# Index queries and keys placed inside SBUF instead of by way of DRAM, in a two-layer hybrid decoder trunk

## The chip, the core and the metric

The kernel runs on one core of a Trainium2 chip. The metric is device time in microseconds (us) of one execution. A core has TensorE (PE: matrix products; its weight loads are shown apart as PEld), VectorE (DVE), ScalarE (ACT), GpSimd (POOL) and SyncE (SP, whose queue issues nearly all transfers here), and sixteen DMA engines that move the data. SBUF is the memory on the core with 128 partitions (rows), PSUM the one that TensorE writes, DRAM the memory outside.

## The reference, cut to what matters

One sequence of 1024 tokens of width 1024 passes two layers. Layer 0 mixes tokens by sparse attention, layer 1 by a short gated convolution; each is followed by a SwiGLU. The part that the change touches is the sparse attention:

```python
q, k = rope(rmsnorm(q)), rope(rmsnorm(k))      # 16 query heads, 4 key heads of 64
qi, ki = rope(qi), rope(layernorm(ki))         # 8 index heads of 64, one index key
s = einsum('bqhd,bsd->bqhs', qi, ki)
score = einsum('bqhs,bqh->bqs', relu(s), wi)   # causal
_, sel = top_k(score, 256)
o = softmax(q . k[sel] / 8) . v[sel]           # per query
```

The rotation (rope) works on the two halves of 32 numbers of each head: `x1*cos - x2*sin` and `x2*cos + x1*sin`. Everything is float32.

## The kernel before, in words

**Who orders the work.** The program is recorded as operations with priorities (`plan.pri`) and costs, and `Plan.drain` (line 392) then acts as a planner: it simulates the five engines and emits, engine by engine, the ready operation of the smallest priority. Each engine executes its own list in that order, so an operation that is late holds all that stand behind it on its engine. Transfers are issued by SP, also in order. `Plan.cost` (line 207) books a transfer from SP at 0.475 us of SP time, or 0.65 us when both ends are SBUF tiles, plus 1.6 us and its bytes at 380 GB/s until it has landed. These are bookings of the planner and no measurements. What depends on what is noted for each tile, or for each named part of a tile (`part_of`). Nearly all instructions are recorded by one helper and bear its line, L244, in the profile, so one goes by tile names.

**Stages.** The attention projections run up to about 311 us, block-wise attention up to about 640 us, and the tail (class `Tail`: feed-forward layers, convolution, output) from there to the end at 2306 us.

**Projections** (`Attention.project`, line 916). Products are made at float32 accuracy from three products of split operands (`whi` and `wlo`, split by ACT and DVE from `raw`, a ring of two weight buffers of 512 KB). `rope_pair` (line 996) makes two PSUM tiles of 128 rows for four heads: tile `two` = 0 has the first halves of the heads (4 heads x 32 rows), tile 1 the second halves, 512 tokens wide (one "half" of the sequence). ACT moves them to SBUF tiles `rt` (a ring of five), and DVE rotates them. The work goes in this order: the index key (`kist`, slot 0 of the tile `karena`), the index queries in four steps (half, pair) = (0,0), (0,1), (1,1), (1,0), the keys for both halves, the queries in four pairs by two halves, the values.

**From the rotated tiles to their places.** A product needs a whole head, 64 numbers, along the partitions, while a rotated tile has 32 rows of each of four heads. So `to_dram` (line 1029) stores the tile in DRAM, 32 rows to each head's place, and a load brings it back:

- Index queries go to `qid` (8 stores of up to 256 KB). `index` (line 1100) loads, for each block of 128 queries from block 2 on, all 8 heads into a half slot of `karena` (slots 1 to 3, 6 loads of 256 KB). It waits for all four stores of its half. The products with `kist` then run for two heads at once (rows 0 to 63 and 64 to 127), ACT takes the positive part from PSUM (`ps_L`) to tiles `s`, and DVE adds them up with their weights to the scores `sc`.
- Keys go to `kd` (4 stores). `load_k` (line 1092) loads them twice, to rows 0 to 63 and to rows 64 to 127 of slots 4 to 7 of `karena` (2 loads of 1 MB), after both halves are stored.
- Queries go to `qd` (16 stores). `attend` (line 1207) loads one block of 128 queries into `qst` (8 loads of 512 KB), one block ahead.

**Selection** (`select`, line 1141) finds the 256th score of each row by a search of 31 steps that ACT (`junk`) or DVE count alternately for two pairs of blocks; the planner puts its steps into gaps of the projections and of attention.

**Attention** (`attend`): for each block and pair of heads, scores on PE, masking and maximum on DVE, exponentials on ACT, transposes and products with values on PE. Beside it run steps of the adaLN projections (`adaw`, 256 KB loads).

**Tail.** `Tail.norm_stat` (line 1415) sums the squares for a norm into a tile `nss` of 4 numbers per partition, from the pool of the `u` tiles. The pool `top` (line 497) holds one unused number per partition at the upper end of SBUF, above the weight pool.

Of the kernel before, what the change touches and what calls it, by code (L numbers as in the profile page):

```python
# [450 lines left out]
P = 128  # L451
# [35 lines left out]
class Trunk:  # L487
# [3 lines left out]
    def __init__(self, plan):  # L491
        self.plan = self.nc = plan
        self.cp = Pool(plan, "const")
        self.pp = Pool(plan, "ps", space=PSUM)
        self.pa = Pool(plan, "pa", space=PSUM)
        self.pg = Pool(plan, "pg", space=PSUM)
        self.top = Pool(plan, "top", side="right")
        self.top.tile([P, 1], F32, name="top")
        self.wp = Pool(plan, "w", side="right", bufs=2)


# [85 lines left out]
    def setup(self, c, positions, ada_b, n1, n2, conv_w, gq, gk, lg, lb, rope_c, arenas, kgb, freq):  # L587
# [2 lines left out]
        nc.gpsimd.memset(ident, 1.0)  # L590
        nc.gpsimd.affine_select(ident, ident, pattern=[[-1, P]], compare_op=ALU.is_equal,
                                fill=0.0, base=0, channel_multiplier=1)
        self.blk4 = cp.tile([P, 4], F32, name="blk4")
        nc.vector.memset(self.blk4, 0.0)
        for i in range(4):
# [161 lines left out]
def trunk_kernel(tc, x, c, positions, ada_w, ada_b, norm1_g, norm2_g, attn_w_in, attn_q_norm_g,  # L757
                 attn_k_norm_g, idx_k_ln_g, idx_k_ln_b, attn_w_out, conv_w_in, conv_w,
                 conv_w_out, ffn_w_gate, ffn_w_up, ffn_w_down, rope_c, out):
    plan = Plan(tc.nc, tc)  # L760
    with ExitStack() as ctx:
        ctx.enter_context(tc.manual_schedule())
        tk = Trunk(plan)
        for p in (tk.cp, tk.pp):
            plan.open(p, ctx)
        xspill = [[plan.wrap(tc.dram_tile([P, HW], F32, name="xs%d_%d" % (i, d)), [P, HW])
                   for d in range(KT)] for i in range(NH)]
        a = Attention(tk, attn_w_in[0], attn_w_out[0], ada_w, xspill)
        a.first_norm(x, positions, lambda v: tk.setup(
            c, positions, ada_b, norm1_g, norm2_g, conv_w, attn_q_norm_g, attn_k_norm_g,  # L770
            idx_k_ln_g, idx_k_ln_b, rope_c, v, a.score[2][:, 256:384], a.score[4][:, HW:HW + 1]))
        a.project()
        a.attend()
        f = Tail(tk, ada_w, xspill)
        a.attended(f)
        f.run(ffn_w_gate, ffn_w_up, ffn_w_down, conv_w_in[0], conv_w_out[0], out)
        right, proj, left = (ctx.enter_context(ExitStack()) for _ in range(3))
        for p in (tk.top, tk.wp):
            plan.open(p, ctx)
        for p, stack in ((tk.pa, left), (a.kp, left), (a.keep, right), (a.sel, right),  # L780
                         (a.hp, proj), (a.pj, proj)):
            plan.open(p, stack)
        plan.drain(a.hp, a.pj)
        proj.close()
        plan.open(a.op, right)
        plan.open(a.at, left)
        plan.drain(a.kp, a.at, tk.pa)
        left.close()
        for p in (tk.pg, *f.first):
            plan.open(p, left)  # L790
        plan.drain(a.keep, a.sel, a.op)
        right.close()
        for p in f.second:
            plan.open(p, left)
        plan.drain()


class Attention:
# [3 lines left out]
    def __init__(self, tk, w, w_out, ada_w, xspill):  # L802
# [4 lines left out]
        def dram(name, shape):  # L807
            return plan.wrap(plan.tc.dram_tile(shape, F32, name=name), shape)

        self.qd = dram("qd", [HEADS * HD, T])  # L810
        self.qid = dram("qid", [IH * HD, T])
        self.kd = dram("kd", [KVH * HD, T])
        self.rd = dram("rd", [2, 4, 32, T // 4])
        self.kp = Pool(plan, "k4")
        self.keep = keep = Pool(plan, "keep", side="right")
# [17 lines left out]

    def arena(self, i):

        return self.karena.part_of(i)[:, i]

    def s4(self):
        return self.sel.tile([P, T], F32, name="s4", tag="s4", bufs=3)
# [76 lines left out]
    def project(self):  # L916
        tk, nc, sp, plan = self.tk, self.nc, self.pj, self.plan
        self.kist = self.arena(0)
        self.ssk = sp.tile([P, TB, KVH], F32, name="ssk", bufs=1)
        self.wiT = sp.tile([P, TB, IH], F32, name="wiT", bufs=1)  # L920
        s = 0
# [12 lines left out]
        for half, j in ((0, 0), (0, 1), (1, 1), (1, 0)):  # L934
            self.unit(s)
            if (half, j) != (1, 1):
                w = tk.wpair(self.w, C_QI + j * 2 * P)
            ts = slice(max(0, FREE_BLK * P - half * HW), HW)
            ab, sl, e = self.rope_pair(w, half, ts, None, None, s)
            s += (e - s) * (ts.stop - ts.start) / HW  # L940
            for two in range(2):
                self.to_dram(ab[two], self.qid, j, two, half, sl)
            if (half, j) == (0, 1):
                ends += self.indexed(s, (2, 3))
        self.free_bias()
# [6 lines left out]
        for half in range(NH):  # L952
# [3 lines left out]
                           self.ssk[:, half * 4:half * 4 + 4].rearrange("p a b -> p (a b)"),  # L956
                           1.0 / HD, sp.tile([P, 64], F32, name="rst", tag="rst8"))
            self.k_out(ab, rk, half, sl)
        self.load_k()
        for j in range(HEADS // 4):  # L960
            self.unit(s)
            w = tk.wpair(self.w, j * 2 * P)
            for half in range(NH):
                ab, sl, s = self.rope_pair(w, half, slice(0, HW), 0,
                                           self.ssq[:, :, 4 * j:4 * j + 4], s)
                for two in range(2):
                    self.to_dram(ab[two], self.qd, j, two, half, sl)
        self.unit(s)
        tk.rsqrt_small(self.qsc.rearrange("p a b -> p (a b)"),
                       self.ssq.rearrange("p a b -> p (a b)"), 1.0 / HD,  # L970
# [55 lines left out]
        tk.rotate(ab, tmp, self.C[:, sl], self.S[:, sl])  # L1026
        return ab, sl, s

    def to_dram(self, t, dram, j, two, half, sl):
        rows = dram.part_of((half, j, two))[2 * P * j:2 * P * (j + 1), sl]  # L1030
        self.nc.sync.dma_start(rows.rearrange("(h a q) t -> a h q t", a=2, q=32)[two], t)


    def ki_chain(self, kw):
        tk, nc, sp = self.tk, self.nc, self.pj
        n = HD + IH
# [43 lines left out]
    def k_out(self, ab, rk, half, sl):  # L1080
# [6 lines left out]
            nc.tensor.transpose(bc[:, blk(i)], rb[:, blk(i)], tk.ident)  # L1087
        for two in range(2):
            nc.vector.tensor_tensor(ab[two], ab[two], bc, op=ALU.mult)
            self.to_dram(ab[two], self.kd, 0, two, half, sl)  # L1090

    def load_k(self):

        src = self.kd.rearrange("(g d) t -> d g t", d=HD)
        dst = self.karena.part_of(list(range(KVH, 2 * KVH)))
        for r in (0, HD):
            self.nc.sync.dma_start(dst[r:r + HD, KVH:], src)


    def index(self, b, n):  # L1100
        tk, nc = self.tk, self.nc
        wd = (b + 1) * P
        q = self.karena.part_of((1 + n // 2, n % 2))[:, 1 + n // 2, half_of(n % 2)].rearrange(
            "p (h t) -> p h t", t=P)
        src = self.qid.part_of([(b // 4, j, two) for j in range(2) for two in range(2)])
        nc.sync.dma_start(q, src[:, blk(b)].rearrange("(h p) t -> p h t", p=P))
        sc = self.score[b]
        for hp in range(IH // 2):
            rs = [self.s4()[:, 0:wd] for _ in range(2)]
            self.pair_products(q[:, hp], self.kist, wd, lambda r, cs, ps: nc.scalar.activation(  # L1110
                rs[r][:, cs], ps, AF.Relu))
            for i, r in enumerate(rs):
                wi = self.wiT[:, b, 2 * hp + i:2 * hp + i + 1]
# [93 lines left out]
    def attend(self):  # L1207
# [4 lines left out]
        for b in range(TB):  # L1212
            if b % 2 == 0:
# [3 lines left out]
            plan.pri = t0 - 12.0  # L1217
            q = (self.at if b % 2 else self.keep).tile([P, T], F32, name="qst", tag="qst",
                                                       bufs=1).rearrange("p (h t) -> p h t", t=P)
            nc.sync.dma_start(q, self.qd[:, blk(b)].rearrange("(h p) t -> p h t", p=P))  # L1220
            for g in range(KVH):
                for _ in range((0, 0, 2, 2, 4, 4, 4, 4)[b]):
                    plan.pri = t0 + (t1 - t0) * g / 4.0
# [133 lines left out]
class Tail:  # L1357
# [57 lines left out]
    def norm_stat(self, half, tag="sm"):  # L1415
# [3 lines left out]
        for d in range(KT):  # L1419
# [2 lines left out]
            if d:  # L1422
                nc.vector.tensor_tensor(sq, acc, sq, op=ALU.add)
            acc = sq
        ps, ss = self.tk.ps(tag), self.up.tile([P, 4], F32, name="nss", tag="nss", bufs=2)
        for t in range(4):
            nc.tensor.transpose(ps[:, blk(t)], acc[:, blk(t)], self.tk.ident)
        nc.vector.tensor_reduce(ss, ps.rearrange("p (a b) -> p a b", b=P), axis=AX.X, op=ALU.add)
# [450 lines left out]
```

## Time and profile before

| what | before |
|---|---|
| median of three runs | 2315.85 us (2315.74 to 2316.34) |
| the profiled execution | 2307.38 us |
| its span, first to last instruction | 2305.7 us |
| mean granted TensorE clock | 0.986 |
| PE / DVE / ACT busy | 96% / 83% / 49% |
| DMA | 356.35 MB, mean 155 GB/s |

The profile shows one execution. A row of a group has the engine, the operation, the tile written and the tiles read, the shape and the count. In brackets stands the time for which the engine sat idle before it, with what ended that wait. Rows of the queue "SPq" are issues of transfers, and their length is that of the issue, not of the transfer. Rows by windows give, for each stretch of time, the busy time of each engine with the number of instructions in brackets, then the granted TensorE clock (1.00 is full speed), the share of the sixteen DMA engines that is busy, and what they move in GB/s. The chain is the sequence of work and waits that ended last, followed back from the end.

### The profile page before, as it was taken

What the parts mean: (1) busy time and instruction counts of PE and PEld (TensorE: products, weight loads), DVE (VectorE), ACT (ScalarE), POOL (GpSimd) and SP (SyncE); (2) the same over time, 40 slices, a digit from 0 to 9 for tenths busy, and PEclk for the clock granted to TensorE, in tenths of its full rate; (3) what the DMA queues carried; (4) which work ended last, traced back from release to release, by engine and by line L of the source; (5) the groups of instructions that cost most, each with busy time, mean ns of one, the idle gap of its engine ahead of it and who ended that gap; (6) DMA issues with size and microseconds to landing.
All of it is one profiled execution on the core that took longest, in us unless ns stands there. A gap on an engine that the chain in (4) does not pass through costs nothing.

```text
span 2305.7 us, 32524 instructions
## 1 busy us (share of the span) xinstructions
PE 2224.8 (96%) x11435; PEld 1777.7 (77%) x11435; DVE 1912.0 (83%) x3851; ACT 1125.6 (49%) x2140; POOL 4.7 (0%) x19
## 2 busy tenths in 40 slices
PE   4989999989999999999999999999999999999998
PEld 2657876766798877888888878778888788888887
DVE  7879999797689888978787999996898877768874
ACT  5476899756755323333444662224553333334444
POOL 0000000000000000000000000000000000000000
PEclk7999999999999999999999999999999999999999
DMA  8323233433345665545983254434446532339724
GB/s 310 116 65 93 89 112 98 137 122 113 120 129 149 191 207 162 180 137 169 349 324 105 100 147 124 119 99 156 129 128 191 161 119 87 124 127 391 286 82 137
DMA packets 334191, 356.35 MB, mean 155 GB/s; under 512 B 18090, under 2 KB 218827, under 8 KB 334027
## 3 DMA queue, kind: packets, MB, share of 16 engines
q1 hardware_dynamic: 333816, 354.14, 47.5%
q8 instruction: 90, 1.47, 0.3%
q14 instruction: 75, 0.61, 0.1%
q10 hardware_dynamic: 210, 0.14, 0.0%
HBM read 282.64 MB, written 71.57 MB: 154 GB/s over the span
## 4 chain that ended last, share of the span: by engine, by line
PE 70%; DVE 13%; DMA 7%; ACT 3%; issue 2%; SPq 0%; ACTq 0%; POOLq 0%; DVEq 0%
PE ps_g L244 40%; PE ps_mm L244 22%; PE ps_sm L244 5%; DVE u L244 2%; DMA raw<-in_conv_w_in_dram 2%; DVE s L244 2%; DVE wlo L244 2%; PE ps_L L244 2%; PE ps_o L244 2%; DMA adaw<-in_ada_w_dram 1%; DVE p L244 1%; ACT p L244 1%; DVE sc L244 1%; DVE v L244 1%; DVE adacc L244 1%
## 5 line engine op out<-in xcount | busy, mean ns | idle before, releaser
L244 ACT CAST whi<-raw 128x512 fp32r<-128x512 f32 (+1 forms) x301 | 184.7, 620 | 410.7 <-PE ps_g L244 158.2
L244 PE MATMUL ps_g<-t,whi 128*128 128x512 f32 x1184 | 369.6, 394 | 2.7 <-DVE whi L244 2.2
L244 ACT CAST whi<-s 128x512 fp32r<-128x512 f32 x276 | 171.1, 621 | 347.2 <-DVE s L244 128.1
L244 PE MATMUL ps_g<-h,whi 128*128 128x512 f32 x1056 | 329.2, 393 | 0.0
L244 DVE TENSOR_TENSOR wlo<-raw,whi 128x512 fp32r<-128x512 f32 (+1 forms) x314 | 214.0, 685 | 84.4 <-ACT whi L244 83.8
L244 PEld LDWEIGHTS ps_g<-t,whi 128*128 128x128 f32 x1184 | 222.8, 189 | 51.7 <-DVE whi L244 3.0
L244 PE MATMUL ps_g<-t,wlo 128*128 128x512 f32 x592 | 232.5, 393 | 1.6 <-DVE wlo L244 1.6
L244 PEld LDWEIGHTS ps_g<-h,whi 128*128 128x128 f32 x1056 | 197.8, 188 | 42.6 <-ACT whi L244 0.4
L244 PE MATMUL ps_g<-h,wlo 128*128 128x512 f32 x528 | 206.3, 391 | 1.2 <-DVE wlo L244 1.2
L244 DVE TENSOR_TENSOR wlo<-s,whi 128x512 fp32r<-128x512 f32 x276 | 188.7, 687 | 19.6 <-ACT whi L244 17.2
L244 PE MATMUL ps_mm<-t,whi 128*128 128x512 f32 x608 | 189.5, 392 | 1.6 <-ACT whi L244 1.6
L244 PE MATMUL ps_g<-ph,whi 128*128 128x512 f32 x572 | 178.2, 392 | 0.0
L244 PEld LDWEIGHTS ps_mm<-t,whi 128*128 128x128 f32 x608 | 114.0, 188 | 26.9 <-ACT whi L244 2.5
L244 PEld LDWEIGHTS ps_g<-t,wlo 128*128 128x128 f32 x592 | 111.5, 188 | 29.4 <-DVE wlo L244 4.8
L244 PEld LDWEIGHTS ps_g<-ph,whi 128*128 128x128 f32 x572 | 107.5, 188 | 23.0
L244 ACT ACTIVATE p<-p,nm,qsc 128x256 f32<-128x256 f32 (+7 forms) x128 | 112.3, 881 | 20.2 <-DVE nm L244 15.2
L244 PE MATMUL ps_mm<-t,wlo 128*128 128x512 f32 x304 | 119.3, 392 | 0.3 <-DVE wlo L244 0.3
L244 PEld LDWEIGHTS ps_g<-h,wlo 128*128 128x128 f32 x528 | 99.1, 188 | 24.1 <-DVE wlo L244 2.1
L244 DVE CUSTOM_DVE_ANT_0 p<-ps_L,bias 128x512 f32<-128x512 f32 (+3 forms) x192 | 99.9, 551 | 21.1 <-PE ps_mm L244 10.4
L244 DVE SCALAR_TENSOR_TENSOR adacc<-adaw,cact,adacc 128x512 f32<-128x512 f32 x140 | 104.7, 748 | 14.5 <-DMA adaw<-in_ada_w_dram 14.1
L244 ACT ACTIVATE junk<-sc,bs 128x896 bf16<-128x896 f32 (+3 forms) x124 | 109.7, 885 | 14.2 <-DVE bs L244 10.9
L244 DVE TENSOR_TENSOR u<-u 128x512 f32<-128x512 f32 x170 | 114.5, 686 | 1.8 <-ACT u L244 0.8
(339 smaller groups left out, 4811.9 us busy)
## 6 DMA issues: line engine op xcount, KB each, us to landing
adaw<-in_ada_w_dram SPq DMA_DIRECT2D x160, 256.0 KB
ph<-in_ffn_w_down_dram SPq DMA_DIRECT2D x66, 512.0 KB
raw<-in_ffn_w_gate_dram SPq DMA_DIRECT2D x54, 512.0 KB
raw<-in_ffn_w_up_dram SPq DMA_DIRECT2D x54, 512.0 KB
raw<-in_conv_w_in_dram SPq DMA_DIRECT2D x34, 512.0 KB
raw<-in_ffn_w_down_dram SPq DMA_DIRECT2D x44, 256.0 KB
ph<-in_ffn_w_down_dram SPq DMA_DIRECT2D x44, 256.0 KB
raw<-in_attn_w_in_dram SPq DMA_DIRECT2D x18, 512.0 KB
```

What stands on the lines that cost most here:

```text
L244: f(*[a.get() if isinstance(a, Ref) else a for a in args], **{k: a.get() if isinstance(a, Ref) else a for k, a in kw.items()})
```

## The change

Five edits, made together:

1. Index queries: each rotated tile of 128 rows is copied inside SBUF by four transfers of 32 rows, straight to the rows of its heads in slots 1 to 3 of `karena`, seen as one tile `qi` of four head pairs by 768 tokens. `index` loads nothing any more; a head pair waits for the four pieces that make it up.
2. Keys: each rotated tile is copied by four transfers of 32 rows to rows 0 to 63 of slots 4 to 7; after the eight pieces of a half, one transfer copies rows 0 to 63 of that half to rows 64 to 127. `load_k` is gone.
3. Queries: `qd` in DRAM is laid out by tiles (half of the head, head, 32 rows, token), so that a store is 128 rows one after the other. A block is loaded by four transfers of 32 rows by 8 heads instead of one.
4. `nss` is one tile among the constants instead of a ring of two in the pool of the `u` tiles.
5. The pool `top` is gone.

```diff
-        self.top = Pool(plan, "top", side="right")
-        self.top.tile([P, 1], F32, name="top")
...
+        self.nss = cp.tile([P, 4], F32, name="nss")
...
-        self.qd = dram("qd", [HEADS * HD, T])
-        self.qid = dram("qid", [IH * HD, T])
-        self.kd = dram("kd", [KVH * HD, T])
+        self.qd = dram("qd", [2, HEADS, 32, T])
...
+        self.qi = self.karena[:, 1:KVH].rearrange("p a t -> p (a t)").rearrange(
+            "p (h t) -> p h t", h=IH // 2)
...
+            at = slice(sl.start - FREE_BLK * P, sl.stop - FREE_BLK * P)
             for two in range(2):
-                self.to_dram(ab[two], self.qid, j, two, half, sl)
+                for h in range(4):
+                    r = (h % 2) * HD + two * 32
+                    nc.sync.dma_start(
+                        self.qi.part_of(("q", half, 2 * j + h // 2, two, h % 2))[
+                            r:r + 32, 2 * j + h // 2, at], ab[two][32 * h:32 * h + 32])
...
-        self.load_k()
...
-                    self.to_dram(ab[two], self.qd, j, two, half, sl)
+                    rows = self.qd.part_of((half, j, two))[two, 4 * j:4 * j + 4, :, sl]
+                    nc.sync.dma_start(rows.rearrange("h q t -> (h q) t"), ab[two])
...
             nc.vector.tensor_tensor(ab[two], ab[two], bc, op=ALU.mult)
-            self.to_dram(ab[two], self.kd, 0, two, half, sl)
+            for g in range(KVH):
+                nc.sync.dma_start(self.karena.part_of(("k", g, half, two))[
+                    32 * two:32 * two + 32, KVH + g, sl], ab[two][32 * g:32 * g + 32])
+        keys = [("k", g, half, two) for g in range(KVH) for two in range(2)]
+        nc.sync.dma_start(self.karena.part_of(("d", half))[HD:, KVH:, sl],
+                          self.karena.part_of(keys)[0:HD, KVH:, sl])
...
-        q = self.karena.part_of((1 + n // 2, n % 2))[:, 1 + n // 2, half_of(n % 2)].rearrange(
-            "p (h t) -> p h t", t=P)
-        src = self.qid.part_of([(b // 4, j, two) for j in range(2) for two in range(2)])
-        nc.sync.dma_start(q, src[:, blk(b)].rearrange("(h p) t -> p h t", p=P))
...
+            q = self.qi.part_of([("q", b // 4, hp, two, r) for two in range(2) for r in range(2)])
-            self.pair_products(q[:, hp], self.kist, wd, lambda r, cs, ps: nc.scalar.activation(
+            self.pair_products(q[:, hp, blk(n)], self.kist, wd,
+                               lambda r, cs, ps: nc.scalar.activation(
...
-            nc.sync.dma_start(q, self.qd[:, blk(b)].rearrange("(h p) t -> p h t", p=P))
+            src = self.qd.rearrange("a (h r) q t -> r a q h t", r=2)
+            for r in range(2):
+                for two in range(2):
+                    at = slice(r * HD + 32 * two, r * HD + 32 * two + 32)
+                    nc.sync.dma_start(q.part_of((r, two))[at], src[r, two, :, :, blk(b)])
...
-        ps, ss = self.tk.ps(tag), self.up.tile([P, 4], F32, name="nss", tag="nss", bufs=2)
+        ps, ss = self.tk.ps(tag), self.tk.nss
```

More of the change, by code (lines that the diff above doesn't have):

```diff
@@ L777, in trunk_kernel @@
         right, proj, left = (ctx.enter_context(ExitStack()) for _ in range(3))
-        for p in (tk.top, tk.wp):
-            plan.open(p, ctx)
+        plan.open(tk.wp, ctx)
         for p, stack in ((tk.pa, left), (a.kp, left), (a.keep, right), (a.sel, right),
@@ L834, in arena @@
     def arena(self, i):
-        return self.karena.part_of(i)[:, i]
+        key = i if i < KVH else [("k", i - KVH, half, two) for half in range(NH)
+                                 for two in range(2)] + [("d", half) for half in range(NH)]
+        return self.karena.part_of(key)[:, i]
     def s4(self):
@@ L1027, in rope_pair @@
         return ab, sl, s
-    def to_dram(self, t, dram, j, two, half, sl):
-        rows = dram.part_of((half, j, two))[2 * P * j:2 * P * (j + 1), sl]
-        self.nc.sync.dma_start(rows.rearrange("(h a q) t -> a h q t", a=2, q=32)[two], t)
     def ki_chain(self, kw):
@@ L1089, in k_out @@
             nc.vector.tensor_tensor(ab[two], ab[two], bc, op=ALU.mult)
-            self.to_dram(ab[two], self.kd, 0, two, half, sl)
[L1092 to L1097, printed above, removed]
+            for g in range(KVH):
[4 more added lines that the diff above has]
+                          self.karena.part_of(keys)[0:HD, KVH:, sl])
     def index(self, b, n):
```

## Prediction, made before the changed kernel was run

> **What bounds the kernel now.** I read the page first, then busy time by stage, the chain of work that ended last, the transfer queue's timeline, and one-microsecond windows around two holes.
>
> ```profile
> span 2305.7 us, 32524 instructions
> ...
> PE 2224.8 (96%) x11435; PEld 1777.7 (77%) x11435; DVE 1912.0 (83%) x3851; ACT 1125.6 (49%) x2140; POOL 4.7 (0%) x19
> ```
>
> ```profile
> 120.00:311.00 191.00, 181.05 (x949) 141.61 (x948) 168.77 (x517) 148.24 (x325) 2.11 (x4) 0.96 0.31 88
> 311.00:400.00 89.00, 82.44 (x670) 51.75 (x669) 84.50 (x317) 85.24 (x241) 0.00 (x0) 0.94 0.31 94
> 400.00:640.00 240.00, 228.30 (x2022) 171.17 (x2023) 182.74 (x549) 165.57 (x330) 0.00 (x0) 1.00 0.38 120
> 640.00:2306.00 1666.00, 1647.43 (x7388) 1352.37 (x7386) 1377.54 (x2270) 665.23 (x1137) 0.00 (x0) 1.00 0.51 166
> ```
>
> The columns are PE, PEld, DVE, ACT, POOL, then granted clock, DMA share, GB/s. The average (PE 96%) is that of the tail, from 640 us on, where PE leaves 18.6 of 1666 us unused and where the change touches almost nothing. It acts in the first row, most of the projections and index scores: PE leaves 10 us there, at a mean clock of 0.96, and VectorE (DVE) 22 us. In the second row, the start of attention, three engines are about equally full. The chain says which waits are behind the idle time of the first row:
>
> ```profile
> 120.73 8.44 DMA qid<-rt
> 129.31 2.78 DMA karena<-qid
> ...
> 208.13 16.25 DMA raw<-in_attn_w_in_dram
> ...
> 234.77 3.08 PE ps_sm L244 x14
> ...
> 290.43 20.97 PE ps_mm L244 x174
> ```
>
> Two transfers of the change's own kind stand in it: the last index queries go out to DRAM (8.44 us) and come back (2.78 us), and later a load of projection weights takes 16.25 us to land. The engines' rows at those places, with the idle time before each in brackets:
>
> ```profile
> 132.13 2.50 PE L244 MATMUL ps_L<-karena 64*128 64x512 f32 x8 [6.17 <-DMA karena<-qid]
> ```
>
> ```profile
> 135.54 0.55 DVE L244 TENSOR_SCALAR sc<-s,wiT 128x640 f32<-128x640 f32 x1 [7.98 <-ACT s L244]
> ```
>
> ```profile
> 224.46 0.62 ACT L244 CAST whi<-raw 128x512 fp32r<-128x512 f32 x1 [4.83 <-DMA raw<-in_attn_w_in_dram]
> ...
> 225.11 0.69 DVE L244 TENSOR_TENSOR wlo<-raw,whi 128x512 fp32r<-128x512 f32 x1 [3.05 <-ACT whi L244]
> ...
> 234.77 1.37 PE L244 MATMUL ps_sm<-blk,qsq 128*128 128x4 f32 x6 [2.52 <-ACT qsq L244]
> ```
>
> In the first hole PE waits for the reload, ACT for PE and DVE for ACT: nothing covers it. In the second, ACT and DVE stand behind the late weights, and ten microseconds later PE stands behind ACT.
>
> **Why the transfers are that slow.** The queue, with start, length of the issues and their number:
>
> ```profile
> 116.19 2.25 SPq L244 DMA_DIRECT2D raw<-in_attn_w_in_dram  x2
> 119.40 1.85 SPq L244 DMA_DIRECT2D qid<-rt  x2
> 129.31 2.02 SPq L244 DMA_DIRECT2D karena<-qid  x4
> ...
> 196.69 1.13 SPq L244 DMA_DIRECT2D kd<-rt  x2
> ...
> 206.10 0.66 SPq L244 DMA_DIRECT2D karena<-kd  x1
> ...
> 207.40 0.62 SPq L244 DMA_DIRECT2D karena<-kd  x1
> 208.13 0.68 SPq L244 DMA_DIRECT2D raw<-in_attn_w_in_dram  x1
> ```
>
> ```profile
> 120.00:121.00 1.00, 1.00 (x6) 0.84 (x5) 0.94 (x4) 0.13 (x1) 0.00 (x0) 1.00 1.01 354
> 121.00:122.00 1.00, 1.00 (x6) 0.81 (x6) 0.00 (x0) 0.97 (x3) 0.00 (x0) 1.00 0.28 49
> ...
> 126.00:127.00 1.00, 0.00 (x0) 0.00 (x0) 0.00 (x1) 0.93 (x4) 0.00 (x0) 1.00 0.26 102
> ...
> 135.00:136.00 1.00, 1.00 (x4) 0.76 (x4) 0.46 (x1) 0.68 (x3) 0.00 (x0) 0.56 0.00 0
> ```
>
> ```profile
> 212.00:213.00 1.00, 1.00 (x6) 0.84 (x5) 1.00 (x7) 0.90 (x2) 0.00 (x0) 1.00 1.07 227
> ...
> 235.00:236.00 1.00, 1.00 (x6) 1.00 (x6) 1.00 (x4) 0.97 (x4) 0.00 (x0) 0.50 0.60 211
> ...
> 240.00:241.00 1.00, 1.00 (x4) 0.81 (x3) 0.93 (x6) 0.97 (x3) 0.00 (x0) 0.50 0.55 181
> ```
>
> Until 121 us two weight loads fill the sixteen DMA engines (354 GB/s). Then the two query stores run at a share of 0.28 to 0.26, four engines of sixteen: 512 KB at 102 GB/s is 5.1 us. Their row pattern has a slowest dimension of four heads, which fits. Around 212 us all engines are busy with the two key loads of 1 MB each, issued at 206.10 and 207.40; at 227 GB/s these 2 MB are 9.2 us, and the weights issued at 208.13 queue behind them.
>
> **The change part by part.** The transfers that it replaces, minimum, median and maximum ns of one issue:
>
> ```profile
> L244 SPq DMA_DIRECT2D qid<-rt x8: 510/516/631, 81.7 to 120.7; - x8
> L244 SPq DMA_DIRECT2D karena<-qid x6: 372/501/507, 93.2 to 130.8; - x6
> ```
>
> ```profile
> L244 SPq DMA_DIRECT2D kd<-rt x4: 516/519/522, 148.3 to 197.3; - x4
> L244 SPq DMA_DIRECT2D karena<-kd x2: 623/644/664, 206.1 to 207.4; - x2
> ```
>
> ```profile
> L244 SPq DMA_DIRECT2D qd<-rt x16: 508/516/5139, 199.4 to 291.8; - x16
> L244 SPq DMA_DIRECT2D qst<-qd x8: 366/378/517, 292.4 to 508.7; - x8
> ```
>
> These 44 issues become 98: 32 query pieces for 14, 16 key pieces and 2 copies for 6, 16 stores and 32 loads for 24. The sum goes part by part.
>
> *Index queries.* The last pair's store and reload, 120.73 to 132.13, becomes eight copies of 32 rows inside SBUF. The first score pair needs pieces one, two, five and six. The first rotated tile is ready at 119.40 (its store is issued then), the second at 120.73. No copy inside SBUF is in the trace. For its issue the nearest rows give 0.366 us (fastest `qst` load) to 0.664 us (slowest key load); I take 0.516, the store of the same tile. For landing after the issue begins I take 2.78 us, the reload above, which is four times the bytes; it could be as little as nothing beyond its 0.366 us of issue. Piece six begins at 119.40 + 5 × 0.516 = 121.98 and lands at 124.8; with 0.664, at 125.5. PE ran out of work at 132.13 − 6.17 = 125.96, so by either price the hole closes. If all eight were needed at the slow price: 119.40 + 7 × 0.664 + 2.78 = 126.8, a wait of 0.9 us. Because the planner may place the scores earlier among PE's work, I keep 0.5 us of wait (0 to 2.5, the other hole's length). The hole had a second price: the clock is at 0.50 from before 132.13 until about 135.9 (0.56 in the row of 135 us), which is half of 3.75 us, 1.9 us. Gain: 6.17 + 1.9 − 0.5 = 7.6 us, 4.2 to 8.1; at the lower end 2.5 us of wait remain and 1.4 of the 1.9 us of clock. Next late is ACT, which clears the scores from PSUM.
>
> *Keys.* Key pieces leave at about 148 and 197 us, and each half's copy to rows 64 to 127 follows. SP's queue is in order, and the copy waits for its eight pieces: behind it stand query stores and the weight load at 208.13. For the second half that is 196.69 + 8 × 0.516 + 2.78 + 0.644, or 204.2; with the slow issue 205.4. That is before 208.13, so nothing waits. The 2 MB read at 206 to 216 is gone, so the weights land in what they need alone: at 354 GB/s 512 KB is 1.5 us; with a landing like the reload's, at most 4.3 us, against 16.25. The weight wait falls by 12 us, but only the holes behind it count: ACT 4.83 us, DVE 3.05, PE 2.52 plus the half clock (0.50 in the six rows from 235 to 240, first and last shown), half of 6 us, 3.0, together 5.5. PE was served by ACT and DVE, which had no other gap there, so I take the mean of their two holes, 3.9 us; bounds 3.05 and 5.5. Next late is DVE's own backlog.
>
> [...]
>
> *Query rows.* The stores now have 128 rows in one dimension; if they use all engines, 2.6 us at 102 GB/s becomes under 1 us. The last is at 291.8 and PE works without a gap until 311, so this is worth 0 us; without that cover at most 1.6. The loads become four per block: 24 more issues at 0.378 is 9.1 us of SP time over the 220 us of attention, loaded a block ahead. Cost 0, at most 9.1 if every one delayed a transfer on the chain.
>
> *Norm sums and the pool "top".* No work added or removed: one slot instead of two, read before the next write. Tiles move by the few bytes freed or taken. Equal operations on tiles of different pools have these means:
>
> ```profile
> L244 DVE TENSOR_TENSOR wlo<-raw,whi 128x512 fp32r<-128x512 f32 (+1 forms) x314 | 214.0, 685 | 84.4 <-ACT whi L244 83.8
> ...
> L244 DVE TENSOR_TENSOR wlo<-s,whi 128x512 fp32r<-128x512 f32 x276 | 188.7, 687 | 19.6 <-ACT whi L244 17.2
> ```
>
> Two ns over all 3851 instructions of DVE are 7.7 us of an engine that is 83% busy: 0 us on the path, at the outside ±2.
>
> Sum: 7.6 + 3.9 = 11.5 us (7.3 to 13.6). The profiled execution, 2307.38 us with 1.68 us around its span, would become 2295.9. The median of the runs shown, 2315.85, lies 8.47 above it; I leave that difference, so 2304.4. A change of 0.2% is 4.6 us, about what a measurement of this kernel can tell from none.
>
> **The rivals.** *Given back in attention.* From 311 to 400 us DVE and ACT are 95 and 96% busy, part of it the threshold search that fills gaps in the projections. A shorter projection stage has fewer gaps, so the search moves into full time. For it: those two shares. Against: ACT and DVE stood still in the very holes that close, so they get the time too. If all of the second part and two thirds of the first go, 2.5 us are left: 2313.3.
>
> *More than the holes.* Every gap of the first row closes (10 us of PE, and 1.9 + 3.0 of half clock: 14.9 us) and attention, where PE idles 18.3 us between 311 and 640, gains some 3 by earlier loads: 2298.0. Against: these waits are on DVE and ACT.
>
> *Slower: the small copies land one after the other.* If each of eight pieces holds the queue for the 2.78 us of a reload, the last queries take 22.2 us instead of 120.73 to 132.13, 11.4; the first hole grows by 10.8, and the second half's key pieces run from 197 to 219 us, so the weights are as late as now: 2326.7. It decides from 1.43 us apiece, where eight equal the old way. Against: the two weight loads at 116.19 did overlap, both moved by 121 us.
> [...] No row here shows a fixed time per transfer that does not overlap.
>
> **How the numbers follow.** Forecast (2301 to 2309, centre 2304.4) 0.60; given back 0.16; more 0.12; one after the other 0.12. So faster by over 0.2% 0.72, within it 0.16, slower 0.12. The planner orders all later work anew from its own bookings (0.65 us for a copy inside SBUF, where 0.475 stood), which can move attention by a part of its 18.3 us of PE gaps either way. The range is therefore 2296 to 2318: it takes in "more" and "given back" and leaves out the slow case and the ends.
>
> **What would show it.** Right: no PE wait over 1 us before the first scores of block 4 and no clock below 0.9 there; weights after the second key half landing within 5 us; `qd` stores above 0.9 of DMA share; attention starting at about 299 us instead of 311. Wrong: score matmuls waiting on the new copies (then the copies are slow or in series), attention starting early but ending where it did (then DVE and ACT bound it), or a projection stage as long as before with DVE full.

## The result, and the profile after

The changed kernel took 2296.28 us (median of five runs, 2293.38 to 2301.77), the kernel before beside it 2315.74 (2306.86 to 2316.34). The ratio taken over all runs is 0.9933, 95% interval 0.9915 to 0.9952, some 15 us (11 to 20); that of the two medians is 0.9916. It is faster, by somewhat more than the forecast 11.5 us, and the time lies at the lower edge of the range. The profiled executions differ by less: 2307.38 us before, 2296.28 after, with spans of 2305.7 and 2294.6. The profiled execution of before was near the fastest of its runs, that of after is the median of its own.

The page's head of the changed kernel (span, then busy time by engine):

```profile
span 2294.6 us, 32635 instructions
...
PE 2217.9 (97%) x11435; PEld 1779.9 (78%) x11435; DVE 1913.8 (83%) x3856; ACT 1123.6 (49%) x2135; POOL 4.2 (0%) x19
```

The same 11435 products keep PE busy for 6.9 us less than before (2224.8). The prediction has only the half clock for that (1.9 and 3.0 us), and the experiments show that the cause is another. By stage, with the columns of before:

```profile
120.00:311.00 191.00, 185.64 (x989) 144.34 (x987) 179.94 (x569) 158.81 (x352) 1.62 (x4) 0.98 0.28 80
311.00:400.00 89.00, 84.85 (x700) 54.26 (x700) 85.17 (x306) 84.47 (x233) 0.00 (x0) 0.97 0.37 102
400.00:640.00 240.00, 228.32 (x2019) 173.56 (x2019) 179.49 (x526) 157.53 (x313) 0.00 (x0) 0.99 0.39 119
640.00:2294.00 1654.00, 1632.62 (x7323) 1346.07 (x7321) 1371.02 (x2257) 661.30 (x1132) 0.00 (x0) 1.00 0.52 167
```

In the first row PE does 40 products more than before (989 for 949), at a clock of 0.98 for 0.96. The place of the first hole, in the transfer queue and on PE:

```profile
116.61 2.26 SPq L244 DMA_DIRECT2D raw<-in_attn_w_in_dram  x2
119.82 26.32 SPq L244 DMA_DIRECT2D karena<-rt  x16
```

```profile
124.93 0.39 PE L244 MATMUL ps_mm<-hhi,wlo 128*128 128x512 f32 x1
125.25 1.35 PE L244 MATMUL ps_L<-karena 64*128 64x512 f32 x8
126.53 0.50 PE L244 MATMUL ps_mm<-hhi,whi 128*128 128x512 f32 x1
```

The score products of block 4 start at 125.25 with no wait in brackets; before they started at 132.13, after 6.17 us. How the small copies move (issue, then windows):

```profile
L244 SPq DMA_DIRECT2D karena<-rt x48: 507/588/1668, 82.1 to 191.1; - x48
...
L244 SPq DMA_DIRECT2D karena<-karena x2: 650/671/692, 147.9 to 193.4; - x2
...
DMA to landing us min/median/max: 1.8/2.0/4.5
```

```profile
122.00:123.00 1.00, 1.00 (x6) 0.84 (x5) 0.13 (x1) 0.97 (x3) 0.00 (x0) 1.00 0.52 137
...
124.00:125.00 1.00, 1.00 (x6) 0.75 (x4) 0.83 (x2) 0.97 (x3) 0.00 (x0) 1.00 0.48 117
```

A copy of 64 KB leaves every 0.588 us and lands 2.0 us after its issue, so three or four are under way at once, at 0.48 to 0.52 of the DMA engines. 65.5 KB in 0.588 us are 111 GB/s, about what the windows show (117 and 137): the issues set the pace.

There is a hole in the changed kernel too, at another place. PE, ACT and the clock there:

```profile
190.20 0.39 PE L244 MATMUL ps_mm<-hhi,wlo 128*128 128x512 f32 x1
193.13 0.51 PE L244 MATMUL ps_mm<-hhi,whi 128*128 128x512 f32 x1 [2.54 <-ACT qsq L244]
193.47 2.63 PE L244 MATMUL ps_sm<-blk,qsq 128*128 128x4 f32 x14
```

```profile
189.61 1.04 ACT L244 ACTIVATE junk<-sc,bs 128x896 bf16<-128x896 f32 x1 [1.10 <-DVE bs L244]
...
190.78 1.15 ACT L244 ACTIVATE junk<-sc,bs 128x1024 bf16<-128x1024 f32 x1
...
191.92 0.67 ACT L244 ACTIVATE rt<-ps_mm,vec 128x512 f32<-128x512 f32 x1
192.49 0.58 ACT L244 ACTIVATE qsq<-ps_mm 128x512 f32<-128x512 f32 x1
```

```profile
193.00:194.00 1.00, 0.87 (x6) 0.82 (x7) 1.00 (x4) 0.85 (x4) 0.00 (x0) 0.92 0.88 148
194.00:195.00 1.00, 1.00 (x6) 1.00 (x6) 1.00 (x3) 0.97 (x3) 0.00 (x0) 0.50 1.07 375
...
200.00:201.00 1.00, 1.00 (x5) 0.82 (x4) 0.97 (x5) 0.47 (x2) 0.00 (x0) 0.66 0.00 0
```

The index scores end about 9 us earlier (last product at 174.93, before 184.02), so the threshold search of blocks 6 and 7 starts earlier as well. Its counts (`junk`) now stand on ACT ahead of the evictions `rt` and `qsq`; the first of the two counts waits 1.10 us for DVE, and PE waits 2.54 us for `qsq`. Then the clock is halved until about 200.7 us. It is as long as the hole that the late weights made before.

To compare runs I take three stretches from each trace. They begin at the first index score (96.5 us before, 97.0 after), because the start-up ahead of it differs by up to 4 us between executions. In us:

| run | edits | first score to start of attention | first score to last product of attention | from there to the end | ratio, 95% interval |
|---|---|---|---|---|---|
| before | none | 214.8 | 533.8 | 1675.4 | 1 |
| after | 1 to 5 | 207.6 | 525.7 | 1671.9 | 0.9933 (0.9915 to 0.9952) |
| e1_queries | 1 | 206.1 | 526.4 | 1677.7 | 0.9968 (0.9955 to 0.9981) |
| e2_keys | 2 | 208.4 | 532.2 | 1678.9 | 0.9988 (0.9976 to 0.9999) |
| e3_rows | 3 | 210.9 | 532.5 | 1675.7 | 0.9977 (0.9965 to 0.9989) |
| e4_nss_top | 4, 5 | 214.5 | 533.0 | 1668.5 | 0.9965 (0.9952 to 0.9978) |
| e5_dram_tiles | other layout | 210.0 | 527.5 | 1676.8 | 0.9959 (0.9940 to 0.9979) |
| e11_no_nss_top | 1 to 3 | 206.1 | 525.7 | 1683.6 | 0.9981 (0.9968 to 0.9995) |
| e12_queries_nss_top | 1, 4, 5 | 206.0 | 522.4 | 1670.1 | 0.9915 (0.9899 to 0.9931) |
| e13_late_search | 1 to 5, search later | 207.7 | 535.2 | 1677.0 | 0.9978 (0.9964 to 0.9992) |

Six kernels (before, e4, e7 to e10) run the same instructions in the same order; their first column goes from 214.0 to 215.6 and their second from 533.0 to 536.3. That is the noise of a single trace. A part of the differences is the clock: the half clock behind the new hole lasts 6.8 us in after and 3.4 in e1, e11 and e12, and after starts attention 1.5 us later than they do. So after gains 7.2 us ahead of attention, keeps them through it (8.1 at its end), and gains 3.5 us more in a tail that the change was not supposed to touch.

### The profile page after: what moved, and what is told of

It reads as the page before. It is cut to its first block, busy times and chain, and to the rows that moved or that the text cites. A ratio compares the mean times of both kernels' runs of the same rounds, so it can differ in the third digit from the quotient of the medians.

```text
span 2294.6 us, 32635 instructions
## 1 busy us (share of the span) xinstructions
PE 2217.9 (97%) x11435; PEld 1779.9 (78%) x11435; DVE 1913.8 (83%) x3856; ACT 1123.6 (49%) x2135; POOL 4.2 (0%) x19
## 4 chain that ended last, share of the span: by engine, by line
PE 66%; DVE 19%; DMA 10%; issue 3%; ACT 1%; SPq 0%; ACTq 0%; DVEq 0%
PE ps_g L244 34%; PE ps_mm L244 24%; PE ps_sm L244 5%; DVE wlo L244 3%; DVE s L244 3%; DVE u L244 3%; PE ps_L L244 3%; DMA raw<-in_conv_w_in_dram 2%; PE ps_o L244 2%; DMA ph<-in_ffn_w_down_dram 2%; DVE v L244 2%; DVE p L244 1%; DMA raw<-in_ffn_w_up_dram 1%; DMA adaw<-in_ada_w_dram 1%; DVE adacc L244 1%
## 5 line engine op out<-in xcount | busy, mean ns | idle before, releaser
L244 ACT ACTIVATE p<-p,nm,qsc 128x128 f32<-128x128 f32 (+7 forms) x128 | 111.3, 871 | 22.5 <-DVE nm L244 20.8
```

The costliest lines, as they stand in the source:

```text
L244: f(*[a.get() if isinstance(a, Ref) else a for a in args], **{k: a.get() if isinstance(a, Ref) else a for k, a in kw.items()})
```

## The experiments

My theory A was the prediction's: the two holes carry the gain. The rival B was that the norm sums and the pool `top` matter, because they move tiles.

### One edit at a time

**e1_queries**: before, with edit 1 of the change alone (the diff is that of `project` and `index` above).

```diff
-                self.to_dram(ab[two], self.qid, j, two, half, sl)
+                for h in range(4):
+                    r = (h % 2) * HD + two * 32
+                    nc.sync.dma_start(
...
+                            r:r + 32, 2 * j + h // 2, at], ab[two][32 * h:32 * h + 32])
...
-        nc.sync.dma_start(q, src[:, blk(b)].rearrange("(h p) t -> p h t", p=P))
```

> Only the index queries go inside SBUF; keys, query rows, norm sums and the pool at the upper end as before. Theory A (the gain is the hole before the first scores of block 4): no PE wait for queries, last score product at 175 us (before: 184.0), first attention scores at about 304.5 us (before: 311.3), time 7 to 11 us under before. Theory B (most of it is the queue freed of the two key loads): attention starts no earlier than 309, time within 4 us of before. Theory C (most of it is the placement of tiles or the tail): within 4 us of before.

2303.29 us, ratio 0.9968. Attention starts 8.7 us earlier, 7.4 of it are left at its end. No wait of PE for index queries is left; the longest between 60 and 320 us is the new hole, so that it comes with the queries and without any change to the keys:

```profile
PE ps_mm L244 <- ACT qsq L244: 2.5, 1, 2.5
```

**e2_keys**: before, with edit 2 alone.

```diff
-            self.to_dram(ab[two], self.kd, 0, two, half, sl)
+            for g in range(KVH):
+                nc.sync.dma_start(self.karena.part_of(("k", g, half, two))[
+                    32 * two:32 * two + 32, KVH + g, sl], ab[two][32 * g:32 * g + 32])
...
+        nc.sync.dma_start(self.karena.part_of(("d", half))[HD:, KVH:, sl],
+                          self.karena.part_of(keys)[0:HD, KVH:, sl])
...
-        self.load_k()
```

> Only the keys go inside SBUF. Theory A: the 6.17 us hole stays, the weights that took 16.25 us land in under 5, but PE's 2.5 us hole behind ACT stays, so attention starts at 309 to 311.3 us and the time is within 4 us of before. Theory B: attention starts 4 to 6 us earlier (305 to 307), time 4 to 8 us under before.

2310.50 us, ratio 0.9988, just distinguishable from 1. By stage and by PE's waits:

```profile
190.00:240.00 50.00, 50.00 (x255) 42.33 (x254) 49.38 (x158) 37.39 (x73) 0.77 (x1) 1.00 0.42 107
```

```profile
PE ps_L L244 <- DMA karena<-qid: 6.1, 1, 6.1
```

The second hole is gone (PE 50.00 of 50.00 us, clock 1.00), the first is as before. Attention starts 6.4 us earlier, more than the 5.5 that the prediction gave as its upper end, but at its last product only 1.6 us are left, within the noise.

**e3_rows**: before, with edit 3 alone.

```diff
-                    self.to_dram(ab[two], self.qd, j, two, half, sl)
+                    rows = self.qd.part_of((half, j, two))[two, 4 * j:4 * j + 4, :, sl]
+                    nc.sync.dma_start(rows.rearrange("h q t -> (h q) t"), ab[two])
```

> Only the query rows in DRAM are laid out by tiles, with four loads per block. Theories A and B: stores of rotated query tiles move at a DMA share near 1 instead of 0.26, attention starts at 311 us as before, time within 4 us of before. A rival: 24 more issues delay the adaLN loads in attention, and the time is 5 to 9 us above before.

2307.14 us, ratio 0.9977. The trace has attention 3.9 us earlier and 1.3 us left at its end. The times show a gain of 0.11 to 0.35%. The trace places the 3.9 us in the second hole. The queue there, before and in e3, and PE's wait in e3:

```profile
208.91 6.73 SPq L244 DMA_DIRECT2D qd<-rt  x2
```

```profile
213.42 1.67 SPq L244 DMA_DIRECT2D qd<-rt  x2
```

```profile
PE ps_sm L244 <- ACT qsq L244: 0.9, 1, 0.9
```

Before, one of these two stores held the queue for 5.14 us. In e3 the late weights land after 14.63 us instead of 16.25, PE's wait for `qsq` falls from 2.52 to 0.9 us, and the clock stays at 1.00 behind it, where it was halved for 6.8 us before and in e4 and e7 to e10. That is 1.6 and 3.4 us, for the 3.9 by which attention starts earlier. Whether the shorter issues or the freed DMA engines bring the weights sooner isn't shown.

**e4_nss_top**: before, with edits 4 and 5 alone. Instructions and their order are those of before; only places change.

```diff
-        self.top.tile([P, 1], F32, name="top")
...
+        self.nss = cp.tile([P, 4], F32, name="nss")
...
-        ps, ss = self.tk.ps(tag), self.up.tile([P, 4], F32, name="nss", tag="nss", bufs=2)
+        ps, ss = self.tk.ps(tag), self.tk.nss
```

> Only the norm sums among the constants and the pool at the upper end gone; every engine has the same instructions in the same order as before. Theories A and B: every stage mark within 1 us of before, time within 4 us of before (what remains is the spread of runs). Theory C: the tail from 640 us on is 3 us or more shorter, time 4 us or more under before.

2303.13 us, ratio 0.9965: as much as the index queries. All of it is in the tail (1668.5 us for 1675.4). Theory A can't account for it; B is right that these edits count, and the next runs ask why.

### Which place matters

**e7_top**: before without the pool `top`; the weight tiles `whi` and `wlo` lie 32 bytes higher.

```diff
-        self.top = Pool(plan, "top", side="right")
-        self.top.tile([P, 1], F32, name="top")
```

> Only the pool at the upper end gone: the weight tiles of the upper side (whi, wlo, raw) lie 32 bytes higher, the tail's operand tiles on the lower side where they were. Theory P1 (the tail's matmuls are slowed by where the operand tiles t, h, ph lie): their start-to-start times stay at a mixture of 226 to 232 ns, mean 228.8, time as before within 4 us. Theory P2 (by where the weight tiles lie): mean 227.0 ns, tail 5 us or more shorter.

**e8_nss**: before with `nss` among the constants; the tail's operand tiles `h`, `t`, `ph` lie 32 bytes lower.

```diff
+        self.nss = cp.tile([P, 4], F32, name="nss")
...
-        ps, ss = self.tk.ps(tag), self.up.tile([P, 4], F32, name="nss", tag="nss", bufs=2)
+        ps, ss = self.tk.ps(tag), self.tk.nss
```

> Only the norm sums among the constants: the tail's operand tiles lie 32 bytes lower, the weight tiles where they were. Theory P1: start-to-start times of the tail's matmuls at 226 to 227 ns, mean 227.0, tail 5 us or more shorter and the time 4 us or more under before. Theory P2: mean 228.8 ns, as before within 4 us.

**e9_pad64**: before with larger `nss` tiles; the operand tiles lie 64 bytes higher.

```diff
-        ps, ss = self.tk.ps(tag), self.up.tile([P, 4], F32, name="nss", tag="nss", bufs=2)
+        ps, ss = self.tk.ps(tag), self.up.tile([P, 12], F32, name="nss", tag="nss",
+                                                   bufs=2)[:, 0:4]
```

> [...] Theory P1 with 64 bytes as the step that matters: mean 228.8 ns, time as before. [...] Theory P2: as before.

All three are slower: 2332.89 us (ratio 1.0096, 1.0068 to 1.0124), 2332.42 (1.0089, 1.0065 to 1.0113) and 2329.29 (1.0087, 1.0056 to 1.0117). So neither half of e4 is the gain, and both theories that I had then (the place of the weights, the place of the operands) fell. What fits all is the distance between the two. The third theory, P3, was tested by a move of the operands alone:

**e10_nss_right**: before, with the norm sums in the tile of the pool `top`; the operand tiles lie 64 bytes lower, and no other tile moves, so that the distance is that of e4 (weights 32 bytes higher, operands 32 lower).

```diff
-        self.top.tile([P, 1], F32, name="top")
+        self.nss = self.top.tile([P, 4], F32, name="top")
...
-        ps, ss = self.tk.ps(tag), self.up.tile([P, 4], F32, name="nss", tag="nss", bufs=2)
+        ps, ss = self.tk.ps(tag), self.tk.nss
```

> The kernel before with one thing changed: the norm sums live in the tile at the upper end of SBUF (that of the pool top, 4 numbers instead of one, which still takes 32 bytes), so that the tail's operand tiles h, t and ph lie 64 bytes lower and nothing else moves; the instructions and their order are those of before. [...] Theory P3 (the difference of the two places sets the pace of the tail's products): PE busy falls from 2224.8 to about 2217.7, the 512-wide products of the tail follow each other at 227.0 ns instead of 228.8, and the time falls by some 8 us, ratio 0.9965. [...] Rival 2 (before happens to be good for its order of tiles, and each move of one side alone costs): pace 232 to 233, PE busy above 2245, ratio 1.009.

2303.68 us, ratio 0.9966 (0.9951 to 0.9981), where P3 gave 0.9965. The pace below is the mean time from the start of one 512-column product of the tail to the start of the next, where they follow each other (0.20 to 0.26 us apart, some 6,850 pairs in each trace):

| distance from operand to weight tiles, against before | runs | pace, ns | PE busy, us |
|---|---|---|---|
| +64 bytes | after, e4, e10, e12, e13 | 226.9 to 227.0 | 2212.6 to 2223.4 |
| 0 | before, e1, e2, e3, e5, e11 | 228.8 to 228.9 | 2224.8 to 2229.4 |
| +32 bytes | e7, e8 | 232.8, 232.7 | 2254.6, 2252.0 |
| -64 bytes | e9 | 232.1 | 2250.3 |

One row of a group shows it on the page, the products of `h` with `whi`: before, in e10 and in e7 (total, then mean ns of one):

```profile
L244 PE MATMUL ps_g<-h,whi 128*128 128x512 f32 x1056 | 329.2, 393 | 0.0
```

```profile
PE 2217.4 (96%) x11435; PEld 1779.8 (77%) x11435; DVE 1911.4 (83%) x3851; ACT 1125.6 (49%) x2140; POOL 4.6 (0%) x19
...
L244 PE MATMUL ps_g<-h,whi 128*128 128x512 f32 x1056 | 326.1, 390 | 0.0
```

```profile
PE 2254.6 (97%) x11435; PEld 1780.0 (76%) x11435; DVE 1915.7 (82%) x3851; ACT 1125.9 (48%) x2140; POOL 4.7 (0%) x19
...
L244 PE MATMUL ps_g<-h,whi 128*128 128x512 f32 x1056 | 333.3, 396 | 0.1
```

393, 390 and 396 ns for the same products (before, e10, e7), at a clock of 1.00 over the tail of before. Runs with one distance and different places (e7 and e8 at 232.8 and 232.7 ns; e4 and e10 within 226.9 to 227.0) have one pace, so it is the distance. All weight tiles (`raw`, `whi`, `wlo`) move together, and so do the operand tiles. So it isn't shown which of these tiles count, or by what.

Some 6,830 products at 1.8 ns less are 12.4 us in after, but its tail is only 3.5 us shorter. Its longer intervals (over 0.26 us from start to start), counted beyond the pace, grew from 22.7 to 32.7 us. About half of this is the clock: after has four stretches of 3.4 us at half clock within the tail and before has one, at 1.7 us each. In e10 the longer intervals are 28.9 us, with two such stretches, and the tail is 6.4 us shorter. PE, DVE and ACT do the tail's work in the same order in all these runs, but for a few neighbours on DVE; why the number of the stretches differs, and whether it is the same in every execution, isn't shown by one trace each.

### The way by DRAM with all engines

**e5_dram_tiles**: before, with the index queries stored in DRAM by tiles (128 rows in one dimension) and loaded by four transfers of 32 rows by 8 heads.

```diff
-        self.qid = dram("qid", [IH * HD, T])
+        self.qid = dram("qid", [2, IH, 32, T])
...
+                rows = self.qid.part_of((half, j, two))[two, 4 * j:4 * j + 4, :, sl]
+                nc.sync.dma_start(rows.rearrange("h q t -> (h q) t"), ab[two])
```

> Index queries still go by way of DRAM, but are stored by tiles as 128 rows in one dimension, and loaded by four transfers of 32 rows per block; all else as before. Theory A1 (the hole was made by stores that use four of sixteen engines): the stores move at a DMA share above 0.8, and PE's 6.2 us hole shrinks to 2 to 3 us. Rival A2 (it is the round trip by DRAM, landing after landing, whatever the rate): the hole stays at 5 us or more.

2302.84 us, ratio 0.9959. The queue, and a window of the stores:

```profile
121.44 1.67 SPq L244 DMA_DIRECT2D qid<-rt  x2
125.72 8.26 SPq L244 DMA_DIRECT2D karena<-qid  x16
```

```profile
123.00:124.00 1.00, 1.00 (x6) 0.81 (x5) 0.02 (x1) 0.97 (x3) 0.00 (x0) 1.00 0.99 370
```

The stores run at 0.99 of the engines, the loads leave 4.28 us after the first store (before: 9.91), and no wait for them is left on PE. So most of the first hole was the old store's share of the engines (0.28 to 0.26), not the way by DRAM as such. Attention starts 4.8 us earlier, 3.9 less than in e1, of which the clock (below) is a part. The intervals of e5 (0.9940 to 0.9979) and e1 (0.9955 to 0.9981) overlap widely, so that the way inside SBUF is better than a better layout in DRAM isn't shown.

### What adds up

**e11_no_nss_top**: the changed kernel without edits 4 and 5.

```diff
-        self.nss = cp.tile([P, 4], F32, name="nss")
+        self.top = Pool(plan, "top", side="right")
+        self.top.tile([P, 1], F32, name="top")
```

> The changed kernel without edits 4 and 5: queries, keys and query rows only, every tile at its place of before. If the result is the sum of what happens ahead of attention and of the pace of the tail: attention starts as in the changed kernel (about 207.6 us after the first index score), PE is busy for about 2226 us, the tail's pace is 228.8 ns, and the time is about 8 us above the changed kernel's, some 2304, ratio 0.9965. Rival (the transfers carry the whole result, and the pace of the tail is given back as other waits): ratio 0.993, as the changed kernel.

2308.09 us, ratio 0.9981: still faster than before, but by less than the sum gave. In the trace, what was gained up to the end of attention (8.1 us) is lost in the tail (1683.6 us for 1675.4), at the same pace of 228.8 ns: the longer intervals, counted beyond the pace, are 31.5 us for 22.7. 5.1 us of this is the clock again, with four stretches at half clock for one. The order of the tail is that of before. PE, ACT and SP have one order in e11 and after, so these two show what edits 4 and 5 are worth in the changed kernel: 0.9981 against 0.9933, some 11 us, with tails of 1683.6 and 1671.9 us.

**e12_queries_nss_top**: the changed kernel without edits 2 and 3.

```diff
-        self.qd = dram("qd", [2, HEADS, 32, T])
+        self.qd = dram("qd", [HEADS * HD, T])
+        self.kd = dram("kd", [KVH * HD, T])
...
+        self.load_k()
```

> The changed kernel without edits 2 and 3: index queries inside SBUF and the two moves of tiles, keys and query rows by DRAM as before. If keys and query rows are worth nothing beside the queries, since the second hole comes back behind ACT in either case: attention starts 206 to 208 us after the first index score, and the time is that of the changed kernel, ratio 0.993. Rival (their single ratios of 0.9988 and 0.9977 add up with the rest): ratio 0.9965, some 8 us above the changed kernel.

2293.63 us (2291.32 to 2295.13), ratio 0.9915. Keys and query rows add nothing beside the queries and the places. Against e1, with the same order of PE and ACT, the two moves of tiles bring it from 0.9968 to 0.9915, as much as between e11 and after. The interval overlaps that of after, so that leaving them out is better isn't shown. It has the lowest time of all that ran.

**e13_late_search**: the changed kernel, with the priorities of the search of blocks 6 and 7 starting 12 us later.

```diff
-        t0, t1 = plan.pri, self.until[pair[0]]
+        t0, t1 = plan.pri + (12.0 if pair[0] == 6 else 0.0), self.until[pair[0]]
```

> The changed kernel, with the threshold search of the last pair of blocks (6 and 7, counted on ACT) given priorities that start 12 us later. Theory (the second hole of the changed kernel, 2.5 us of PE at 190.6 and the lower clock after it, stands behind search counts that the planner put ahead of the eviction to qsq): the hole goes, attention starts about 4 us earlier (203 to 204 us after the first index score), and if attention doesn't give it back the ratio is 0.9915. Rival 1 (VectorE's backlog of score sums delays the eviction whatever ACT counts): the hole stays, ratio 0.993. Rival 2 (the search then runs in attention's full time): attention starts earlier, but its last product is no earlier than 525 us after the first score, ratio 0.993 or above.

2307.64 us, ratio 0.9978. The hole stayed, behind the same counts. PE, then ACT:

```profile
195.16 0.50 PE L244 MATMUL ps_mm<-hhi,whi 128*128 128x512 f32 x1 [2.52 <-ACT qsq L244]
```

```profile
191.64 1.04 ACT L244 ACTIVATE junk<-sc,bs 128x896 bf16<-128x896 f32 x1 [1.09 <-DVE bs L244]
```

The start-up took 2.0 us more in this run, so these times are the same as in after: the edit did not move the counts at this place, and what it was to test stays open there. A likely reason, not tried, is that the planner fills an idle engine with what is ready whatever its priority. Later it did act: attention ends 9.5 us later than in after.

## Why the prediction was right, and where it was wrong

- **Base.** Against the profiled execution the sum gave 2295.9 us; the profiled execution of after is 2296.28. The 8.47 us that were added for the median fit before alone: the profiled execution of after is its median. The terms of the sum were not all those of the result, though:
- **Index queries, 7.6 us (4.2 to 8.1): right.** e1 has 8.7 us at the start of attention and 7.4 at its end, though it holds the new second hole as well. The hole closed with its half clock; a piece cost 0.588 us of issue, between the ends of 0.366 and 0.664.
- **"Slower: the small copies land one after the other": refuted.** The condition was 1.43 us apiece; a copy left every 0.588 us, and the landings overlap. The 2.0 us to landing (1.8 at least, 2.0 in the median) are a delay of each copy and not a time that they add up. Many small transfers in the place of one large one cost PE nothing here: the engines were half used (0.48 to 0.52), and the scores of block 4 started with no wait at 125.25.
- **Keys, 3.9 us (3.05 to 5.5): the step that failed in the changed kernel.** Alone they close the hole (e2). Beside the queries the term was 0: e1, with the old keys, starts attention as early as e11 with the new ones (206.1 both). The two holes were priced as if independent, but when the scores end earlier, search counts stand in front of the key evictions. That order is in the traces; that it alone makes the new hole isn't shown, since e13 didn't move the counts. The weights after the second key half did land early, in 3.6 us. The prediction named the next late ("DVE's own backlog") and gave it no price.
- **Query rows, 0: wrong by themselves, right beside the others.** The step priced only the last store, at 291.8, under PE's cover. It passed over the stores that run beside the late weights, among them one whose issue takes 5.14 us (the maximum of 5139 ns in its own row); alone the edit brings 0.11 to 0.35% (e3). Beside the queries the old second hole is gone, and no gain is left (e12).
- **"Norm sums and the pool top: 0 us on the path, at the outside ±2": wrong.** Together they are worth 0.22 to 0.48% (e4), some 5 to 11 us, and in the changed kernel 0.48% (e11 against after); each alone costs 0.6 to 1.2%. The step looked at places, but only at DVE's rows. PE, busy for 99% of the tail (1647.43 of 1666 us in the row of before), was the engine to price.
- **Given back in attention, and more than the holes: neither there.** The lead of 7.2 us at the start of attention was 8.1 at its end. Attention starts at 304.6 instead of the predicted 299, since a second hole remains. But something is given back in the tail, which no rival named: edits 1 to 3 without the moves (e11) have the same 8.1 us at the end of attention and a ratio of 0.9981.
- **Clock: the row was read rightly.** The prediction put the half clock (0.50 in its rows from 235 us on) down to the 2.52 us without a product. The end of PE's work before this hole, and the clock at its end, in before:

```profile
231.86 0.39 PE L244 MATMUL ps_mm<-hhi,whi 128*128 128x512 f32 x1
```

```profile
234.00:235.00 1.00, 0.23 (x2) 0.23 (x2) 1.00 (x3) 1.00 (x3) 0.00 (x0) 0.94 0.91 315
```

The last product ends at 232.25, and the clock falls at about 234.9 (0.94 over the us from 234), 2.6 us later. In after it falls at about 193.8 (0.92 over the us from 193), behind an idle time of 2.54 us and one full product. e2, which closes the hole, starts attention 6.4 us earlier, more than the wait of 2.52 us without a half clock would give.

So the size of the gain was right by chance. What the prediction gave a price, edits 1 to 3, brings 0.05 to 0.32% (e11), some 1 to 7 us for a forecast of 11.5 (7.3 to 13.6). A loss (keys, and what the tail gives back) and a gain that was not foreseen (places, some 11 us) nearly cancel.

## What to carry to other kernels

When two waits follow each other, price the second after the first is gone: what comes earlier fills the engine that the second step needs (here search counts stood ahead of the eviction on ACT, and PE waited 2.54 us for it). Before moving a transfer off DRAM, see how many DMA engines its pattern uses; a layout with 128 rows in the outer dimension, at 0.99 of the engines for 0.28 to 0.26, closed the same hole. And an edit that "only" moves tiles by some bytes has to be timed alone: here it was worth between -0.5 and +1.0%, more than the transfers that the change was made for (-0.2% without it).

## What the runs showed of the hardware

**In these runs the pace of the tail's products went with the distance between weight tiles and operand tiles.** 226.9 to 232.8 ns from start to start for the same float32 products of 512 columns, by moves of 32 to 64 bytes; the granted clock over the tail is 1.00 in before (228.8 ns) and in after (227.0). Against the distance of before, +64 bytes gave 226.9 to 227.0 ns, +32 gave 232.8 and 232.7, and -64 gave 232.1. That +32 is worse than 0 shows that nearer to the good distance isn't better by itself. Only these four distances were run; what they have to do with the pace isn't shown.

**In e5 the clock fell without a gap on PE.** PE and the clock there:

```profile
130.47 0.39 PE L244 MATMUL ps_sm<-blk,qsq 128*128 128x4 f32 x2
130.72 0.48 PE L244 MATMUL ps_mm<-hhi,whi 128*128 128x512 f32 x1
131.03 1.62 PE L244 MATMUL ps_sm<-blk,qsq 128*128 128x4 f32 x14
132.58 1.90 PE L244 MATMUL ps_L<-karena 64*128 64x512 f32 x8
```

```profile
133.00:134.00 1.00, 1.00 (x6) 0.38 (x4) 0.99 (x4) 0.00 (x0) 0.00 (x0) 0.62 0.26 71
134.00:135.00 1.00, 1.00 (x7) 0.69 (x4) 0.17 (x1) 0.90 (x2) 0.00 (x0) 0.50 0.44 126
...
136.00:137.00 1.00, 1.00 (x4) 0.52 (x2) 1.00 (x3) 0.97 (x4) 0.00 (x0) 0.67 0.00 0
```

PE shows 1.00 busy throughout, but from 130.47 to 132.58 it worked almost only on products of four columns, with score products of 64 rows on both sides. The clock was halved from about 133.2 to 136.6. So a busy PE row (1.00 of the us from 134) stood beside a clock of 0.50; how little work lets it fall isn't shown. The stretches at half clock, in order of time and ahead of the last few us, measure 30.7, 3.4, 6.8, 6.8, 10.2 and 3.4 us in the trace of before, and 30.7, 3.4, 6.8, 6.8 and then five times 3.4 us in that of after.
